# Eight experts on one core: the order of TensorE, ScalarE and VectorE written down, column-tile products side by side, weight splits one step ahead

## The chip, the core and the metric

One core of a Trainium2 chip runs the whole program. The metric is the device time of one execution in microseconds (us), lower is better. The kernel is one launch: two layers of a network on 256 tokens of width 1024. Layer 0 ends in a dense feed-forward net, layer 1 in eight experts. The change touches the experts alone.

## The reference, cut to what matters

```python
def moe_swiglu(h, w_router, w_up, w_down):            # h: 256 tokens x 1024
    logits = jnp.einsum('td,de->te', hf, w_router)
    top_logit, top_e = lax.top_k(logits, 2)           # two of eight experts for each token
    top_gate = jax.nn.softmax(top_logit, axis=-1)
    ...
    gate, up = jnp.split(h_pad[tok] @ w_up[e], 2, axis=-1)   # w_up[e]: 1024 x 7168
    return (jax.nn.silu(gate) * up) @ w_down[e]              # w_down[e]: 3584 x 1024
    ...
    out = zeros.at[slot_tok].add(slot_gate * y)
```

All weights are float32, and each expert's are read once: 8 x 42 parts of 1 MB.

## The kernel before

**Turns and blocks.** The experts are sorted by their number of tokens into turns 0 to 7. Turns 0, 1 and 2 have 128 rows (turn 1 up to 32 more, its "overflow"), turn 3 has 64, turns 4 to 7 have 32. A turn is 14 blocks of 256 hidden channels, and a block has three weight parts of 1 MB: two for the up product (U), one for the down product (D). Between U and D stands the gate step (G): silu times up, and a transpose through PSUM.

**The ring.** SyncE fetches the parts (`fetch`, L894) into a ring of ten 1 MB buffers in the order of `plan` (L887). The fetch of part n+10 waits until part n's buffer is free.

**Many rows (turns 0 to 2).** TensorE works with float32r, so a part is split in two halves into a high and a low piece: ScalarE copies (L257), VectorE subtracts (L258). A half goes into one of six pair buffers (`pairs`). Each product is then three matmuls (`mm3`, L252 to L254): 24 for a U, 12 for a D. A ring buffer is free once its part has been split. G transposes (L826) into the one PSUM bank `pb`, and `split` takes it from there.

**Few rows (turns 3 to 7 and the overflow).** The tokens are the stationary operand in column tiles of 32 or 64 (L1053 for U, L1075 and L1079 for D), and the weights stream unsplit in float32. A ring buffer is free only after its product. ScalarE takes U out of PSUM (L1055), TensorE transposes it into `pb` (L1062), ScalarE and VectorE gate it (L1066, L1067).

**The order.** `lanes_merged` mixes the blocks of the two lanes into one list of 112, mostly one many block (M) and then one or two few blocks (f): M f f M f M f f. `steps` (L1119 to L1138) does at step k, whatever the lane: U of block k, G of block k-1, D of block k-2, then `tick(2)`. A tick advances a queue of side jobs: `rows` gathers the next turn's tokens (VectorE L994, TensorE L1001, and L296 and L294 out of PSUM), `back` prepares its scatter matrix (L1014, L1018, L1020), and `scatter` adds a finished turn into x (TensorE L1040 into the one bank `pc`, VectorE L1042). In a scatter one tick adds the last product and issues the next one, which needs that bank. Before its scatter, `taken_out` (L1031) moves the turn's sums out of PSUM.

**Who sets each engine's order.** The whole of `lanes` is traced inside `manual_schedule` for TensorE alone: TensorE executes in the order of the trace. ScalarE and VectorE are ordered by the framework's scheduler. Each engine then works its list strictly in order.

Of the kernel before, what the change touches and what calls it, by code (L numbers as in the profile page):

```python
# [152 lines left out]
def trunk(tc, a, dbg=None):  # L153
# [83 lines left out]
    def halves(w, name, at=None):  # L237
        out = []
        for j in range(2):
            wj = w[:, 1024 * j:1024 * j + 1024]  # L240
            if at is not None:
                pair = pairs[taken[0] % PAIRS]
                taken[0] += 1
            else:
                pair = work.tile([P, 2, 1024], F32R, name=f"{name}{j}", tag="wp", bufs=count["wp"])
            with tc.issue_after(held.pop(0).ins) if held else ExitStack():
                split(pair[:, 0], pair[:, 1], wj)
            out.append((pair[:, 0], pair[:, 1]))
        return out

# [126 lines left out]
    def norm_affine(l, j, xn, scale=1.0):  # L377

        for q in range(2):
            n = slice(512 * q, 512 * q + 512)  # L380
            wb = []
            for r in range(2):
                t = base.tile([P, 512], F32, name="lnr", tag="lnr", bufs=2)
# [431 lines left out]
    def glu_products(ws, x_):  # L815
        p = bank("pa")
        for i, w in enumerate(ws):
            for k in (2 * i, 2 * i + 1):
                wh, wl = [t[:, 512 * (k % 2):512 * (k % 2) + 512] for t in w]
                mm3(p, *x_(k), wh, wl, k == 0, k == KD - 1)  # L820
        return glu_gate(p)

# [43 lines left out]
    def parts_in(order):  # L866
        for k in range(len(order) + 2):
            if k < len(order):
                yield from ((*order[k], i) for i in range(2))
            if k >= 2:  # L870
                yield (*order[k - 2], 2)
# [11 lines left out]

    def one_by_one():
        return [p for q in range(NE) for p in parts_in(blocks_of(q))]

    plan = list(parts_in(lanes_merged()))  # L887
    assert all(q == 0 for q, _, _ in plan[:RING]) and plan[:RING] == one_by_one()[:RING]
    ring, pairs, who, taken = [], [], [], [0]
# [11 lines left out]
    def moe(xn, cw, cb, g2):  # L901
# [87 lines left out]
        def rows(q, r, n, xe, xr, tag="pc"):  # L989

            rank, ind, _ = of_turn(q, r)
            sel = work.tile([P, NB, P], F32, name="sel")
# [14 lines left out]
        def back(q, r, n, pT):  # L1007
# [4 lines left out]
            wgt = work.tile([P, NB, P], F32, name="wgt")  # L1012
# [13 lines left out]
        def taken_out(n, ac):  # L1026

            ys = [base.tile([P, 512], F32, name="y_e", tag="lnr", bufs=2) for _ in range(2)] if n == P else [work.tile([P, 512], F32, name="y_f", bufs=2)] * 2
# [14 lines left out]


        def tiled_sums(n, ws, xr):

            m = P // n
            w = 512 // m
            ps = bank("pa")
# [4 lines left out]
            s = s2("pk", "aff")[:, 0:w]  # L1054
            A.copy(s, ps[:, 0:w])  # L1055
# [26 lines left out]
        def split_part(q, f, i):  # L1082

            n = plan.index((q, f, i))
            return ahead[n] if n in ahead else halves(ring[n % RING], "wup" if i < 2 else "mdn", True)

        def over_with(q, f, i):

            n = plan.index((q, f, i))
            if n + RING < len(plan):  # L1090
                fetch(n + RING)

        def used(q, f, which, parts, do):

            split_ = [w for i in which for w in split_part(q, f, i)] if any(p[0] == P for p in parts) else None
            tiled = any(p[0] < P for p in parts)
            if not tiled:
                for i in which:
                    over_with(q, f, i)
            tiles = [ring[plan.index((q, f, i)) % RING] for i in which]  # L1100
            out = [do(p, split_ if p[0] == P else tiles) for p in parts]
            if tiled:
                for i in which:
                    over_with(q, f, i)
            return out

        def steps(order, parts, at=lambda *step: None):


            taken[0] = 2 * AHEAD  # L1110
            ups, gs = {}, {}

            def up(p, ws):
                return glu_products(ws, lambda k: (p[1][:, k, :, 0], p[1][:, k, :, 1])) if p[0] == P else tiled_sums(p[0], ws, p[1])

            def gate_(q, u):
                return [glu_finish(v) if p[0] == P else tiled_gate(p[0], v) for p, v in zip(parts[q], u)]

            for k in range(len(order) + 2):  # L1119
                if k < len(order):  # L1120
# [5 lines left out]
                if k >= 2:  # L1126
                    q, f = order[k - 2]
                    of_part = {id(p): g for p, g in zip(parts[q], gs.pop(k - 2))}

                    def down(p, ws):  # L1130
                        if p[0] == P:
                            glu_down(p[2], of_part[id(p)], ws, f == 0, f == NEB - 1)
                        else:
                            tiled_down(p[0], p[2][0], of_part[id(p)], ws[0], f == 0, f == NEB - 1)
# [32 lines left out]
        def lanes():  # L1167

            order = lanes_merged()
# [12 lines left out]

            def at(step, q, f):
                lane = MANY if q in MANY else FEW
                if step == "up" and f == 0:
                    while coming.get(q) in queue:
                        tick()
                if step == "up" and f == 2 and q != lane[-1]:
                    prepare_turn(lane[lane.index(q) + 1])
                if step == "done" and f == NEB - 1 and order[-1] != (q, f):  # L1190
                    for i, (n, _, ac) in enumerate(parts[q]):
                        queue.append(scatter(n, taken_out(n, ac), pTo if i else place_of(q)[2]))

            prepare_turn(FEW[0])
            steps(order, parts, at)
            drain()
            q = order[-1][0]
            n, _, ac = parts[q][0]
            finish(n, taken_out(n, ac), place_of(q)[2])
# [26 lines left out]
        def alone(q, *ns):  # L1226
# [7 lines left out]
            steps(blocks_of(q), {q: parts})  # L1234
# [31 lines left out]
        ahead = {}  # L1266
        ahead.update({n: split_part(*plan[n]) for n in range(AHEAD)})
# [81 lines left out]
```

## Time and profile before

| | us |
|---|---|
| median of 3 runs | 1569.8 |
| lowest, highest | 1563.7, 1571.1 |
| profiled execution, its time | 1567.5 |
| profiled execution, span of the trace | 1565.7 |

Busy over the span: TensorE matmuls 86%, weight loads 64%, VectorE 60%, ScalarE 41%. Mean granted TensorE clock: 0.93 of full speed. Fetched: 481 MB. The profiled execution lies 1.8 us over its span and 2.3 us under the median. Matmuls are pipelined, so one that is recorded with 0.39 us can follow its neighbour after 0.23 us; a busy share of TensorE is therefore no measure of what is left. "A <- B" means that A waited for B.

### The profile page before, as it was taken

What the parts mean: (1) busy time and instruction counts of PE and PEld (TensorE: products, weight loads), DVE (VectorE), ACT (ScalarE), POOL (GpSimd) and SP (SyncE); (2) the same over time, 40 slices, a digit from 0 to 9 for tenths busy, and PEclk for the clock granted to TensorE, in tenths of its full rate; (3) what the DMA queues carried; (4) which work ended last, traced back from release to release, by engine and by line L of the source; (5) the groups of instructions that cost most, each with busy time, mean ns of one, the idle gap of its engine ahead of it and who ended that gap; (6) DMA issues with size and microseconds to landing.
All of it is one profiled execution on the core that took longest, in us unless ns stands there. A gap on an engine that the chain in (4) does not pass through costs nothing.

```text
span 1565.7 us, 26221 instructions
## 1 busy us (share of the span) xinstructions
PE 1351.9 (86%) x10468; PEld 1002.7 (64%) x10468; DVE 933.4 (60%) x1756; ACT 640.8 (41%) x1138; POOL 52.5 (3%) x44
## 2 busy tenths in 40 slices
PE   2799878999799997999989888888888898888884
PEld 2688756887688876776655656555656466655551
DVE  6799897888789968853433434344434544443433
ACT  2648733443465853652332323323423324433410
POOL 0000040000040003000000000000000000000000
PEclk9799979999989996999998898999999899989886
DMA  9772447889555215888999878897999989999994
GB/s 351 294 265 73 162 144 288 332 338 352 212 188 165 78 47 196 310 309 336 420 419 395 323 308 335 361 404 302 369 392 392 405 317 420 418 418 420 418 419 197
DMA packets 68755, 481.07 MB, mean 307 GB/s; under 512 B 8720, under 2 KB 8848, under 8 KB 11152
## 3 DMA queue, kind: packets, MB, share of 16 engines
q1 hardware_dynamic: 66672, 473.61, 76.7%
q0 software_dynamic: 960, 3.15, 0.7%
q10 hardware_dynamic: 992, 2.56, 0.4%
q8 instruction: 84, 1.38, 0.4%
q14 instruction: 47, 0.39, 0.1%
HBM read 478.23 MB, written 1.05 MB: 306 GB/s over the span
## 4 chain that ended last, share of the span: by engine, by line
PE 64%; DVE 16%; DMA 12%; ACT 5%; issue 3%; ACTq 0%; DVEq 0%; SPq 0%
PE pa L1053 10%; PE pa L253 7%; PE pa L254 7%; PE pa L252 7%; PE acc L253 5%; PE acc L254 5%; PE acc L252 4%; DMA rawb<-m_dn 4%; PE acc L1075 3%; DVE pair L258 3%; DMA rawb<-m_up 3%; DMA ring<-m_up 3%; DVE wada L327 2%; PE pc L1040 2%; PE pc L1001 2%
## 5 line engine op out<-in xcount | busy, mean ns | idle before, releaser
L258 DVE TENSOR_TENSOR pair<-rawb,pair 128x1024 fp32r<-128x1024 f32 x152 | 177.6, 1221 | 18.6 <-ACT pair L257 17.6
L257 ACT CAST pair<-rawb 128x1024 fp32r<-128x1024 f32 x152 | 149.4, 1048 | 14.0 <-DMA rawb<-m_up 4.6
L252 PE MATMUL pa<-pair,xe 128*128 128x512 f32 x336 | 141.1, 420 | 7.1 <-ACT xef L294 4.8
L253 PE MATMUL pa<-pair,xe 128*128 128x512 f32 x336 | 139.1, 414 | 6.5 <-DVE pair L258 6.5
L1055 ACT COPY pk<-pa 128x128 f32<-128x128 f32 (+1 forms) x84 | 23.8, 284 | 293.7 <-PE pa L1053 293.7
L254 PE MATMUL pa<-pair,xe 128*128 128x512 f32 x336 | 137.0, 408 | 0.0
L811 ACT ACTIVATE g_act<-pa 128x256 f32<-128x256 f32 x64 | 24.6, 385 | 245.6 <-PE pa L254 245.6
L258 DVE TENSOR_TENSOR pair<-ring,pair 128x1024 fp32r<-128x1024 f32 x100 | 117.0, 1223 | 12.0 <-ACT pair L257 11.9
L327 DVE CUSTOM_DVE_ANT_0 wada<-wada,sc 128x1024 f32<-128x1024 f32 x96 | 115.1, 1220 | 3.8 <-DMA wada<-w_ada 3.7
L258 DVE TENSOR_TENSOR g_l<-pb,g_h 128x256 fp32r<-128x256 f32 x64 | 27.1, 424 | 145.7 <-ACT g_h L257 145.6
L252 PE MATMUL acc<-pair,g_h 128*128 128x512 f32 x168 | 80.6, 480 | 35.5 <-ACT pair L257 35.5
L812 DVE TENSOR_TENSOR g_act<-g_act,pa 128x256 f32<-128x256 f32 x64 | 26.8, 419 | 136.6 <-ACT g_act L811 136.3
L257 ACT CAST pair<-ring 128x1024 fp32r<-128x1024 f32 x100 | 98.2, 1048 | 20.3 <-DVE rs_y L273 11.8
L1053 PE MATMUL pa<-rawb,xl 128*32 128x128 f32 (+1 forms) x2336 | 101.0, 294 | 1.4 <-DMA rawb<-m_up 1.4
L1053 PEld LDWEIGHTS pa<-rawb,xl 128*32 128x32 f32 (+1 forms) x2336 | 79.1, 116 | 35.1 <-issue 23.1
L253 PE MATMUL acc<-pair,g_h 128*128 128x512 f32 x168 | 82.2, 489 | 20.7 <-DVE pair L258 20.7
L1067 DVE TENSOR_TENSOR pk_g<-pk_g,pb 128x64 f32<-128x64 f32 (+1 forms) x84 | 19.3, 230 | 126.5 <-ACT pk_g L1066 126.5
L252 PEld LDWEIGHTS pa<-pair,xe 128*128 128x128 f32 x336 | 68.7, 204 | 36.2 <-ACT pair L257 12.6
L253 PEld LDWEIGHTS pa<-pair,xe 128*128 128x128 f32 x336 | 68.3, 203 | 23.1 <-DVE pair L258 9.2
L254 PE MATMUL acc<-pair,g_l 128*128 128x512 f32 x168 | 77.5, 461 | 0.0
L254 PEld LDWEIGHTS pa<-pair,xe 128*128 128x128 f32 x336 | 68.3, 203 | 14.1
L1053 PE MATMUL pa<-ring,xl 128*32 128x128 f32 (+1 forms) x1696 | 70.5, 296 | 6.6 <-DMA ring<-m_up 6.6
(320 smaller groups left out, 2838.4 us busy)
## 6 DMA issues: line engine op xcount, KB each, us to landing
rawb<-m_up SPq DMA_DIRECT2D x132, 1024.0 KB, 9.9
ring<-m_up SPq DMA_DIRECT2D x92, 1024.0 KB, 10.2
rawb<-m_dn SPq DMA_DIRECT2D x68, 1024.0 KB, 12.0
wada<-w_ada SPq DMA_DIRECT2D x48, 1024.0 KB, 6.6
ring<-m_dn SPq DMA_DIRECT2D x44, 1024.0 KB, 11.5
win<-w_in SPq DMA_DIRECT2D x24, 1024.0 KB, 5.3
wup<-f_up SPq DMA_DIRECT2D x22, 1024.0 KB, 5.8
fdn<-f_dn SPq DMA_DIRECT2D x11, 1024.0 KB, 6.0
```

The costliest lines, as they stand in the source:

```text
L252: T.matmul(ps, xh, wh, start=first, stop=False)
L253: T.matmul(ps, xh, wl, start=False, stop=False)
L254: T.matmul(ps, xl, wh, start=False, stop=last)
L257: A.copy(h, src)
L258: return V.tensor_sub(lo, src, h.bitcast(F32))
L327: V.tensor_tensor_reduce(wi, wi, sc, 1.0, 0.0, ALU.mult, ALU.add, c[:, i:i + 1])
L811: A.activation(g, p[:, 0:FB], AF.Silu)
L812: V.tensor_mul(g, g, p[:, FB:2 * FB])
L1001: T.matmul(ps[:, k * n:(k + 1) * n], xn[b][:, kk * P:(kk + 1) * P], sel[:, b, 0:n], start=b == 0, stop=b == NB - 1)
L1040: T.matmul(ps, pT[p, b], ys[h][p], start=True, stop=True)
L1053: T.matmul(ps[n * i:n * i + n, 0:w], xr[:, k], ws[k // 4][:, c:c + w], start=k == 0, stop=k == KD - 1)
L1075: T.matmul(ac[n * i:n * i + n], g[:, j], wd[:, D * j + 512 * h:D * j + 512 * h + 512], start=first, stop=last)
```

## The change

- The order of the work inside a step is written out by `in_lanes` as a program of (step, U/G/D, turn, block, part). In an f step it is: G of the last few block, G and U of the overflow, U of the new few block, D of the last few block and of the overflow, and then at its end the many lane's D and G if they are due. All column-tile products of a step then stand together. In an M step: the many lane's U, and those of its G and D that are due.
- `plan`, the fetch order, follows the new program: a few part D moves up by up to three places, many parts down by one.
- `split_until` emits the splits for the *next* step's many products right behind a U, ahead of the ScalarE step that takes that U out of PSUM, as far as the six pair buffers are free. The fetch into a split part's buffer is then also issued earlier.
- `manual_schedule` covers TensorE, ScalarE and VectorE: all three execute in traced order.
- One tick at the start of a step, and one more ahead of a many U, in place of two at the end of each step. A finished turn's scatter is queued only if at most three result buffers are in use; else ticks are run on the spot.
- Buffers: tag `lnr` has 3 instead of 2 and also holds `y_f`; `sel` and `wgt` share one buffer; the taken-out U has a tag of its own.

```diff
+    def in_lanes():
+        got = {w + k: [] for w in "UGD" for k in "mfo"}
...
+        for s in range(len(order) + 2):
+            q, f = order[s] if s < len(order) else (None, None)
+            if q in MANY:
...
+                put_(s, "U", "m")
+                fresh, got["Gm"] = got["Gm"], gated
+                put_(s, "G", "m")
+                later, got["Dm"] = got["Dm"], ready
+                put_(s, "D", "m")
...
+            else:
+                put_(s, "G", "f")
+                put_(s, "G", "o")
+                put_(s, "U", "o")
...
+                put_(s, "U", "f")
+                put_(s, "D", "f")
+                put_(s, "D", "o")
+                put_(s, "D", "m")
+                put_(s, "G", "m")
...
-            for k in range(len(order) + 2):
-                if k < len(order):
-                    q, f = order[k]
...
-                    ups[k] = used(q, f, (0, 1), parts[q], up)
-                if 1 <= k <= len(order):
-                    gs[k - 1] = gate_(order[k - 1][0], ups.pop(k - 1))
...
-                    used(q, f, (2,), parts[q], down)
-                    at("done", q, f)
-                tick(2)
+            def split_until(step, o):
+                while left[1] < len(todo):
+                    t = left[1]
+                    n, j, first, _ = todo[t]
+                    if program[first][0] > step or t >= PAIRS and todo[t - PAIRS][3] > o:
+                        return
+                    if t == len(ahead):
+                        ahead.append(half(ring[n % RING], j, pairs[t % PAIRS]))
...
+                    if j:
+                        released(n, [p for p in uses[n] if many(program[p])])
...
+                if what == "U":
+                    split_until(s + 1, o)
+                    sums[q, f, r] = glu_gate(ps) if n == P else tiled_take(ps)
...
+                if step == "next":
+                    tick()
+                elif step == "done":
+                    if q != end:
+                        n, _, ac = parts[q][f]
+                        while sum(u for t, u in sums if t in queue) + (2 if n == P else 1) > 3:
+                            tick()
...
+                    if q in MANY:
                         tick()
...
-            with tc.manual_schedule(engines={mybir.EngineType.PE}):
+            with tc.manual_schedule(engines={mybir.EngineType.PE, mybir.EngineType.Activation, mybir.EngineType.DVE}):
                 lanes()
```

## Rows read from the trace of the kernel before

**Rows 1.** Busy time by stage: us, busy of each engine, granted clock, DMA share, GB/s.

```profile
core 0: us, PE busy (x) PEld busy (x) DVE busy (x) ACT busy (x) POOL busy (x), PEclk, DMA share, GB/s
660.00:720.00 60.00, 57.18 (x344) 41.06 (x345) 27.39 (x50) 23.11 (x39) 0.00 (x0) 0.94 0.72 276
720.00:860.00 140.00, 130.30 (x759) 83.18 (x761) 51.93 (x64) 44.85 (x72) 0.00 (x0) 0.96 1.00 411
860.00:1000.00 140.00, 121.52 (x1304) 83.35 (x1301) 61.75 (x89) 48.37 (x84) 0.00 (x0) 0.91 0.81 321
1000.00:1060.00 60.00, 52.44 (x676) 35.58 (x674) 20.64 (x29) 16.72 (x32) 0.00 (x0) 0.94 0.99 403
1060.00:1080.00 20.00, 17.16 (x136) 10.86 (x132) 9.06 (x11) 6.83 (x11) 0.00 (x0) 0.91 0.51 187
1080.00:1220.00 140.00, 120.76 (x1577) 84.14 (x1568) 55.33 (x78) 51.02 (x93) 0.00 (x0) 0.97 0.96 390
1220.00:1300.00 80.00, 70.31 (x560) 44.73 (x560) 40.89 (x56) 25.48 (x41) 0.00 (x0) 0.92 0.92 363
1300.00:1543.00 243.00, 202.36 (x2119) 139.37 (x2117) 95.86 (x122) 78.03 (x131) 0.00 (x0) 0.89 1.01 417
```

**Rows 2.** Chain that ended last, its end: start us, us, what.

```profile
1523.77 19.33 DMA rawb<-m_dn
1543.23 1.10 PE acc L1075 x8
```

**Rows 3.** Waits of PE from 860 to 1300 us: us in total, times, longest.

```profile
PE acc L252 <- ACT pair L257: 16.6, 13, 1.5
PE pb L1062 <- DVE g_l L258: 12.9, 14, 0.9
PE acc L253 <- DVE pair L258: 11.7, 23, 0.8
PE pc L1040 <- DVE x L1042: 8.7, 10, 1.2
PE pa L253 <- DVE pair L258: 4.6, 5, 1.6
```

**Rows 4.** Timeline of ACT and PE, one many D: start us, us, [idle before].

```profile
1130.09 0.27 ACT L1055 COPY pk<-pa 128x128 f32<-128x128 f32 x1 [2.60 <-PE pa L1053]
1130.38 5.77 ACT L257 CAST pair<-rawb 128x1024 fp32r<-128x1024 f32 x6
1131.47 0.49 PE L252 MATMUL acc<-pair,g_h 128*128 128x512 f32 x1 [1.25 <-ACT pair L257]
1132.73 0.50 PE L253 MATMUL acc<-pair,g_h 128*128 128x512 f32 x1 [0.77 <-DVE pair L258]
1133.07 0.40 PE L254 MATMUL acc<-pair,g_l 128*128 128x512 f32 x1
1136.25 0.63 PE L253 MATMUL acc<-pair,g_h 128*128 128x512 f32 x1
```

**Rows 5.** Timeline of PE, two few steps between many products.

```profile
1146.38 1.07 PE L1075 MATMUL acc<-rawb,pk_g 128*32 128x512 f32 x8
1147.26 1.93 PE L1053 MATMUL pa<-rawb,xl 128*32 128x128 f32 x64
1149.12 0.44 PE L826 MATMUL pb<-small,g_act 128*128 128x128 f32 x2
```

**Rows 6.** Timeline: a D before a transpose, a many U's gate, a few block's gate.

```profile
1104.89 1.06 PE L1075 MATMUL acc<-ring,pk_g 128*32 128x512 f32 x8
1105.89 0.44 PE L1018 MATMUL pc<-small,wgt 128*128 128x128 f32 x2
1102.42 0.40 PE L254 MATMUL pa<-pair,xe 128*128 128x512 f32 x1
1103.27 0.42 DVE L812 TENSOR_TENSOR g_act<-g_act,pa 128x256 f32<-128x256 f32 x1 [2.88 <-ACT g_act L811]
1109.50 0.33 PE L1062 MATMUL pb<-small,pk 128*128 128x128 f32 x1 [0.92 <-DVE g_l L258]
1110.12 0.22 DVE L1067 TENSOR_TENSOR pk_g<-pk_g,pb 128x64 f32<-128x64 f32 x1 [0.68 <-ACT pk_g L1066]
```

**Rows 7.** DVE and ACT groups, 860 to 1300 us: busy, mean ns, idle before.

```profile
L258 DVE TENSOR_TENSOR pair<-rawb,pair 128x1024 fp32r<-128x1024 f32 x72 | 83.7, 1221 | 6.6 <-ACT pair L257 6.6
L1042 DVE TENSOR_TENSOR x<-x,pc 128x512 f32<-128x512 f32 x23 | 15.8, 687 | 26.0 <-PE pc L1040 25.9
L257 ACT CAST pair<-rawb 128x1024 fp32r<-128x1024 f32 x72 | 69.9, 1047 | 0.0
```

**Rows 8.** Timeline of PE, two scatter products in one pair of ticks.

```profile
1254.84 1.12 PE L1040 MATMUL pc<-y_f,pTo 64*128 64x512 f32 x2
1256.75 1.12 PE L1040 MATMUL pc<-y_f,pTo 64*128 64x512 f32 x2 [0.78 <-DVE x L1042]
```

More of the change, by code (lines that the diff above doesn't have):

```diff
@@ L235, in trunk, with halves, half @@
     held = []
-    def halves(w, name, at=None):
+    def halves(w, name):
         out = []
         for j in range(2):
[L240 to L248, printed above, removed]
-        return out
+            out.append(half(w, j, work.tile([P, 2, 1024], F32R, name=f"{name}{j}", tag="wp", bufs=count["wp"])))
+        return out
+    def half(w, j, pair):
+        with tc.issue_after(held.pop(0).ins) if held else ExitStack():
+            split(pair[:, 0], pair[:, 1], w[:, 1024 * j:1024 * j + 1024])
+        return pair[:, 0], pair[:, 1]
     def mm3(ps, xh, xl, wh, wl, first, last):
@@ L813, in glu_gate @@
         return g
[L815 to L821, printed above, removed]
     def glu_finish(g):
@@ L991, in rows @@
             rank, ind, _ = of_turn(q, r)
-            sel = work.tile([P, NB, P], F32, name="sel")
+            sel = work.tile([P, NB, P], F32, name="sel", tag="sel")
             for b in range(NB):
@@ L1026, in taken_out @@
         def taken_out(n, ac):
-            ys = [base.tile([P, 512], F32, name="y_e", tag="lnr", bufs=2) for _ in range(2)] if n == P else [work.tile([P, 512], F32, name="y_f", bufs=2)] * 2
+            ys = [base.tile([P, 512], F32, name="y_e", tag="lnr", bufs=3) for _ in range(2 if n == P else 1)]
+            ys = [ys[0], ys[-1]]
             for h in range(2):
@@ L1053, in tiled_sums, with tiled_take @@
                     T.matmul(ps[n * i:n * i + n, 0:w], xr[:, k], ws[k // 4][:, c:c + w], start=k == 0, stop=k == KD - 1)
-            s = s2("pk", "aff")[:, 0:w]
-            A.copy(s, ps[:, 0:w])
+            return ps[:, 0:w]
+        def tiled_take(ps):
+            s = work.tile([P, 256], F32, name="pk", bufs=2)[:, 0:ps.shape[1]]
+            A.copy(s, ps)
             return s
@@ L1080, in tiled_down @@
                                  start=first and j == 0, stop=last and j == 1)
[L1082 to L1105, printed above, removed]
@@ L1181, in prepare_turn @@
                     queue.append(coming[q])
+            sums = []
+            program = in_lanes()
+            end = program[-1][2]
             def at(step, q, f):
                 lane = MANY if q in MANY else FEW
-                if step == "up" and f == 0:
-                    while coming.get(q) in queue:
-                        tick()
[L1188 to L1192, printed above, removed]
+                if step == "next":
[5 more added lines that the diff above has]
+                            tick()
+                        sums.append((scatter(n, taken_out(n, ac), pTo if f else place_of(q)[2]), 2 if n == P else 1))
+                        queue.append(sums[-1][0])
+                else:
+                    if f == 0:
+                        while coming.get(q) in queue:
+                            tick()
+                    if f == 2 and q != lane[-1]:
+                        prepare_turn(lane[lane.index(q) + 1])
+                    if q in MANY:
+                        tick()
             prepare_turn(FEW[0])
-            steps(order, parts, at)
+            run(program, parts, at)
             drain()
-            q = order[-1][0]
-            n, _, ac = parts[q][0]
-            finish(n, taken_out(n, ac), place_of(q)[2])
+            n, _, ac = parts[end][0]
+            finish(n, taken_out(n, ac), place_of(end)[2])
         def finish(n=None, ys=None, pT=None):
@@ L1233, in alone @@
                 parts.append((n, to, accs[2 * r:2 * r + 2]))
-            steps(blocks_of(q), {q: parts})
+            run(in_turn(q, len(ns)), {q: parts})
             for (n, _, ac), pT in zip(parts, pTs):
@@ L1265, in moe @@
             pass
-        ahead = {}
-        ahead.update({n: split_part(*plan[n]) for n in range(AHEAD)})
+        first = [half(ring[t // 2], t % 2, pairs[t]) for t in range(2 * AHEAD)]
         take_turns()
         with tc.If(nc.values_load(cnt[0:1, 0, 0:1], min_val=0, max_val=1) > 0) as c:
-            with tc.manual_schedule(engines={mybir.EngineType.PE}):
+            with tc.manual_schedule(engines={mybir.EngineType.PE, mybir.EngineType.Activation, mybir.EngineType.DVE}):
                 lanes()
```

118 lines of the change are left out of this document (89 added, 29 removed).

## The prediction, made before the changed kernel was run

> **What bounds the kernel now.** I began with the stages [rows 1]. What to look at there is the rate of the fetches, not TensorE's busy share. From 1300 us on the fetch engines are full: 417 GB/s, DMA share 1.01. The chain of waits agrees: at its end it stands on one part's flight of 19.33 us, and the last few D starts 0.13 us after that lands [rows 2]. A part of 1.05 MB takes 2.51 us at 417 GB/s, so some eight parts are then under way at once, which is nearly the whole ring. In that stretch nothing that TensorE does faster can shorten the run. From 720 to 860 us it is the same, at 411 GB/s. From 860 to 1300 us it is not: the five stages move (140 x 321 + 60 x 403 + 20 x 187 + 140 x 390 + 80 x 363) / 440 = 356 GB/s [rows 1]. There the ring waits for its buffers, and so for TensorE, ScalarE and VectorE. At 417 GB/s the same bytes would need 440 x 356 / 417 = 376 us. **The room is 64 us**, and the change has to earn its gain from 860 to 1300 us. From 660 to 720 us the rate is low too (276 GB/s), but there TensorE is busy for 57.2 of 60 us, and the change removes no product; I count nothing.
>
> What TensorE waits for in the 440 us [rows 3] is mainly the splits: 16.6 us for ScalarE's copy and 11.7 us for VectorE's subtraction ahead of a many D, 4.6 us ahead of a U. One such place stands in [rows 4]. ScalarE stands idle for 2.60 us because its next instruction is the take-out of a few U, which isn't finished. Six weight copies are queued behind it. They start at 1130.38, and TensorE gets its first matmul of D at 1131.47, 1.25 us late, and the second 0.77 us late. The matmuls that followed at 0.40 us are then recorded at 0.63 us: the granted clock has fallen, which in these stages leaves it at 0.91 to 0.97 of full [rows 1], a mixture of 2.4 and 1.2 GHz.
>
> **The change, part by part,** from 860 to 1300 us, which in the list of 112 is about steps 32 to 79, with 18 many blocks.
>
> *Splits a step ahead, gain.* The copies now stand ahead of the take-out, so ScalarE works in the 2.60 us in which it was idle. The data are not the obstacle: outside the full stretches the parts have landed. I take all 16.6 + 11.7 + 4.6 = 33 us away. The splits stay beside TensorE's work: four halves need 4 x 1.22 us on VectorE [rows 7], and a few step with a many D lasts about 6 us.
>
> *Clock, gain.* (1 - clock) x length summed over the five stages is 12.6 + 3.6 + 1.8 + 4.2 + 6.4 = 29 us of lost pulses [rows 1]. Between nothing (the new waits below lower the clock as well) and 29 us, I take two thirds, 19 us, since the fall in [rows 4] follows just such a split wait.
>
> *Column-tile products side by side, gain.* From a few D to a column-tile U the start-to-start time is 0.88 us [rows 5], from a few D to a transpose over the whole array it is 1.00 us [rows 6]. A change of tiling thus costs 0.12 us. An M f f group had eight of them and will have four: 18 x 4 x 0.12 = 9 us.
>
> *One bank `pb`, cost.* G of the overflow now stands right behind G of a few block, and both use `pb`. Such a transpose starts at 1109.50, lasts 0.33 us, and VectorE has emptied the bank at 1110.34 [rows 6]: 0.5 us of waiting, 14 times, 7 us. The known wait for `pb` behind a many G (0.92 us, 12.9 us in all [rows 3]) stays where an f follows, and goes in the 4 blocks of turn 1 where an M follows: 3.7 us. Net 3 us.
>
> *Side jobs, cost; the term I know least.* In a tick TensorE waits for VectorE's addition before it may write `pc` again. Now that addition stands in the traced order behind everything of the step before, the next step's splits included. Behind a many U: its last matmul ends at 1102.82, the gate at 1103.69 [rows 6], the addition takes 0.69 us [rows 7], so 1.6 us. Behind a many G: 0.92 + 0.69 = 1.6 us. In the pair of ticks ahead of a many U: 0.78 us, as now [rows 8]. Worst is an M step behind a single f, where six splits stand in front: 1.05 + 6 x 1.22 us, then the many G's subtraction and the addition, some 10 us after the f step began, against 3.5 to 5.4 us that TensorE needs for it (D and U 0.88 and 1.86 us, start to start [rows 5]): 6.4 or 4.5 us. Written out, the steps in which a scatter is under way have five pairs (3.9), four ticks behind a U (6.2), one behind a G (1.6), three behind four splits (about 2), a run of forced ticks when turn 5 ends (2) and two of the worst kind (10.9): 27 us against 8.7 us now [rows 3], so 18 us more. For the five gathers I take 4 us more, between 0 and 8 (1.6 us each). Sum 22 us. From below it is nothing, if VectorE has run ahead; from above see the last rival.
>
> *Take-out behind the splits, cost.* In an M behind a single f of turn 1, the overflow's take-out now comes after six copies (6 x 1.05 us [rows 7]), and U waits for its PSUM bank: about 1.7 us, three times (the fourth is inside a tick's wait): 5 us.
>
> *At nothing:* the few D part fetched up to three places earlier is also used one step earlier; SyncE's earlier issues only lengthen its lead; the third `lnr` buffer serves GpSimd ahead of the experts; the end after the last landing is unchanged. When the fetches are the limit, a copy that waits for a part in flight now holds up the take-out and the next G. At most six landed parts then lie unused, and four of ten stay under way, still more than one at a time: cover enough.
>
> **Sum.** 33 + 19 + 9 = 61 us gained, 3 + 22 + 5 = 30 us lost, 31 us net. From 1000 to 1060 us the fetches are full already (0.99), 60 of 440 us, so I keep 86%: 27 us. The profiled execution's 1567.5 us (its span 1565.7 us and 1.8 us around it) less 27 is 1540.5; its 2.3 us to the median are within the spread of the runs. I forecast 1540 us.
>
> A rule that speaks against the change: the Trainium skill, "DMA: Bandwidth & Descriptors", section "Where 436 GB/s comes from", says that a transfer from HBM is bound at about 358 GB/s for each core. By it the 356 GB/s from 860 to 1300 us would be the limit already, the gain nothing and the time 1567 us, the second rival below. The trace speaks against it with 417 GB/s for 243 us [rows 1], so it adds no chance there.
>
> **Rivals.** *The whole room is won.* If VectorE and ScalarE run far enough ahead that the ticks cost no more than now, 61 - 3 - 5 = 53 us are there, and buffers freed a step earlier smooth the rest: at most 64 us, 1503 us. For it: VectorE is busy for 188 of the 440 us [rows 1]. Against it: six splits in one f step exceed that step. Chance 0.2, at 1503 to 1520.
>
> *Nothing is left.* The clock is not regained (19 us less) and the gathers cost their 8 us: 27 - 19 - 4 = 4 us, 1563 us; or the mean wait of a tick is 3 us. Chance 0.2, at 1562 to 1577.
>
> *Slower: VectorE's written order.* The side jobs' additions and affines outside the full stretches are some 20 on which TensorE waits. My sum has about 1.7 us for each. If four splits (4.9 us) stand in front each time, it is 20 x 3.2 = 64 us more: 1604 us. It decides from a mean of 1.7 + 27 / 20 = 3.0 us on. For it: in the old order the scheduler could put these short jobs first, and a split ahead may also wait for its part. Against it: ScalarE and VectorE stand idle for more than half of these stages. Chance 0.15, at 1578 to 1605.
>
> **How the numbers follow.** The forecast has 0.45, by itself 1525 to 1560. A measurement here tells 0.5%, about 8 us, from no change: the borders are 1562 and 1578. Faster is forecast and first rival, 0.65; same 0.2; slower 0.15. The range 1508 to 1590 leaves out about half of the first and of the last rival.
>
> **What would show it.** Right: from 860 to 1300 us the waits of a many D for the splits under 5 us in all (33 with U now), a rate above 375 GB/s, the granted clock at 0.95 or more, and the last landing near 1516 us. The waits of L1040 for L1042 grow, from 8.7 to some 27 us, the longest 4 to 6 us in an M step behind a single f; a wait of L1062 for L1067 of 0.5 us appears 14 times. Wrong: split waits that stay, or a rate under 356 GB/s; a full rate from 860 us on is the first rival, waits of L1040 and L1001 above 50 us in all are the last.

## The result, and the profile after

The changed kernel takes **1583.7 us** (median of 4 runs, 1582.2 to 1592.5) against 1567.3 us for the kernel before beside it: a ratio of 1.0116 with a 95% interval of 1.0069 to 1.0163. It is slower by 1.2%, where I had forecast 27 us faster. The time lies inside the range; the direction is wrong.

Line numbers have moved: splits are L254 (ScalarE) and L255 (VectorE), the scatter L1077 (TensorE) and L1079 (VectorE), the gather L1037, L293 and L291, a many G L815, a few U L1095, its take-out L1100, a few D L1120, a few block's transpose L1107 and its gate L1112. First the stages of the changed kernel, with the columns of [rows 1] and one stage more in front:

```profile
580.00:660.00 80.00, 65.24 (x293) 56.02 (x292) 57.70 (x137) 34.19 (x50) 13.08 (x10) 0.81 0.59 227
660.00:720.00 60.00, 57.70 (x324) 42.97 (x324) 28.86 (x45) 25.16 (x39) 0.00 (x0) 0.91 0.70 270
720.00:860.00 140.00, 130.28 (x791) 85.58 (x785) 59.05 (x75) 49.59 (x80) 0.00 (x0) 0.96 0.96 392
860.00:1000.00 140.00, 115.25 (x1262) 85.90 (x1266) 57.17 (x87) 44.76 (x82) 0.00 (x0) 0.90 0.83 333
1000.00:1060.00 60.00, 51.78 (x682) 38.19 (x674) 25.68 (x32) 21.36 (x38) 0.00 (x0) 0.94 0.99 406
1060.00:1080.00 20.00, 17.08 (x145) 10.76 (x149) 7.57 (x11) 4.99 (x9) 0.00 (x0) 1.00 0.99 407
1080.00:1220.00 140.00, 116.15 (x1556) 88.42 (x1548) 55.41 (x78) 48.63 (x89) 0.00 (x0) 0.94 0.92 372
1220.00:1300.00 80.00, 64.82 (x494) 40.84 (x498) 33.09 (x46) 20.14 (x33) 0.00 (x0) 0.83 0.81 325
1300.00:1543.00 243.00, 196.13 (x2039) 143.31 (x2028) 100.31 (x131) 80.45 (x137) 0.00 (x0) 0.88 0.99 407
```

The first of these stages in the kernel before, which I had not looked at:

```profile
580.00:660.00 80.00, 68.15 (x323) 58.74 (x321) 68.24 (x149) 40.98 (x57) 15.25 (x12) 0.85 0.69 262
```

Read as bytes, length times rate, the account closes (it has to, both kernels fetch the same parts); what it shows is where the bytes fall behind. From 580 to 860 us 89.2 MB came in against 95.1 MB before: 5.8 MB less, 14 us at 417 GB/s. From 860 to 1300 us it is 157.2 against 156.5 MB, a gain of not 2 us. From 1300 to 1543 us it is 407 against 417 GB/s, 2.4 MB or 6 us less. Together 18 us behind, and the last part lands 16.6 us later: at 1559.68 us, by the end of the chain of waits, against 1543.10 us [rows 2].

```profile
1542.20 17.48 DMA rawb<-m_dn
```

The waits of TensorE from 860 to 1300 us (us in total, times, longest) have changed their kind:

```profile
PE pc L1077 <- DVE x L1079: 27.9, 15, 6.0
PE pb L1107 <- DVE g_l L255: 21.6, 9, 6.1
PE pb L1107 <- DVE pk_g L1112: 8.2, 14, 0.8
PE pa L249 <- ACT pk L1100: 6.0, 3, 3.1
PE pc L1037 <- ACT xl L291: 3.1, 2, 1.6
```

No wait for a split is left (they were 33 us in [rows 3]). In its place stand the scatters (first line), `pb` behind a many G (second), and the small ones. One scatter of the worst kind, an M step behind a single f, in the timelines of VectorE, ScalarE and TensorE:

```profile
1273.46 2.36 DVE L255 TENSOR_TENSOR pair<-ring,pair 128x1024 fp32r<-128x1024 f32 x2 [0.71 <-ACT pair L254]
1275.74 4.62 DVE L255 TENSOR_TENSOR pair<-rawb,pair 128x1024 fp32r<-128x1024 f32 x4
1280.28 0.41 DVE L255 TENSOR_TENSOR g_l<-pb,g_h 128x256 fp32r<-128x256 f32 x1
1280.62 0.67 DVE L1079 TENSOR_TENSOR x<-x,pc 128x512 f32<-128x512 f32 x1
...
1274.28 3.88 ACT L254 CAST pair<-rawb 128x1024 fp32r<-128x1024 f32 x4
1278.06 0.26 ACT L1100 COPY pk<-pa 128x128 f32<-128x128 f32 x1
...
1274.91 0.44 PE L815 MATMUL pb<-small,g_act 128*128 128x128 f32 x2
1281.35 2.07 PE L1077 MATMUL pc<-y_e,pTl 64*128 64x512 f32 x2 [6.00 <-DVE x L1079]
1284.20 2.07 PE L1077 MATMUL pc<-y_e,pTl 64*128 64x512 f32 x2 [0.78 <-DVE x L1079]
1286.80 0.63 PE L250 MATMUL pa<-pair,xe 128*128 128x512 f32 x1
```

The addition that frees `pc` has had its operand since 1271.98 us (the product started at 1270.86 and lasted 1.12 us), but in the written order it stands behind six splits and the G's subtraction. TensorE stands for 6.00 us, and when it goes on it has lost its clock too: the product takes 2.07 us where [rows 8] has 1.12, and the first matmuls of U 0.63 instead of 0.39 us.

Something like it stands at the very start, where I had counted nothing. TensorE in the changed kernel, the two gather products around the first many U:

```profile
623.07 3.65 PE L1037 MATMUL pc<-sel,ln_xh 128*128 128x64 f32 x16 [3.43 <-DVE sel L1030]
636.09 3.57 PE L1037 MATMUL pc<-sel,ln_xh 128*128 128x64 f32 x16 [2.44 <-ACT xl L291]
```

In the kernel before, both stand without a wait and take 1.89 and 1.90 us (from 629.47 and 637.09 us), though its first many U has itself waited 4.82 us. In the run f3 below, in which the VectorE work for them stands elsewhere, they take as little:

```profile
629.78 1.89 PE L1037 MATMUL pc<-sel,ln_xh 128*128 128x64 f32 x16
637.39 1.90 PE L1037 MATMUL pc<-sel,ln_xh 128*128 128x64 f32 x16
```

Bytes run ahead of the work by up to a ring, so here is the work itself, by VectorE's gates of the 42 many blocks (L812 before, L809 after). The change is 17.4 us behind at the eighth (762.4 against 745.0 us), but only 2.4 us at the 28th, and 24.7 us at the last (1523.0 against 1498.3 us). The 28th, before and after:

```profile
1207.79 0.42 DVE L812 TENSOR_TENSOR g_act<-g_act,pa 128x256 f32<-128x256 f32 x1 [4.89 <-ACT g_act L811]
1210.23 0.42 DVE L809 TENSOR_TENSOR g_act<-g_act,pa 128x256 f32<-128x256 f32 x1 [8.42 <-ACT g_act L808]
```

So the change makes up what it lost at the start, and loses it again behind 1210 us: from 1220 to 1300 us the scatters wait 14.5 us, from 1300 to 1400 us `pb` waits 14.1 us behind a many G.

### The profile page after: what moved, and what is told of

Read it like the earlier page. It is cut to its first block, busy times and chain, and to the rows that moved or that the text cites. A ratio compares the mean times of both kernels' runs of the same rounds, so it can differ in the third digit from the quotient of the medians.

```text
span 1582.6 us, 26217 instructions
## 1 busy us (share of the span) xinstructions
PE 1336.1 (84%) x10468; PEld 1018.7 (64%) x10468; DVE 929.9 (59%) x1756; ACT 635.4 (40%) x1138; POOL 51.7 (3%) x44
## 4 chain that ended last, share of the span: by engine, by line
PE 57%; DVE 19%; DMA 15%; ACT 6%; issue 3%; ACTq 0%; DVEq 0%
PE pa L1095 8%; DMA rawb<-m_dn 8%; PE pa L249 6%; PE pa L250 6%; PE pa L251 6%; DMA ring<-m_dn 5%; DVE pair L255 5%; PE acc L249 4%; PE acc L250 4%; PE acc L251 4%; PE pc L1037 2%; PE acc L1120 2%; ACT pair L254 2%; DVE wada L324 2%; PE pc L1077 2%
## 5 line engine op out<-in xcount | busy, mean ns | idle before, releaser
L255 DVE TENSOR_TENSOR pair<-rawb,pair 128x1024 fp32r<-128x1024 f32 x150 | 174.7, 1219 | 63.2 <-ACT pair L254 63.1
L809 DVE TENSOR_TENSOR g_act<-g_act,pa 128x256 f32<-128x256 f32 x64 | 26.7, 418 | 282.7 <-ACT g_act L808 282.5
L254 ACT CAST pair<-rawb 128x1024 fp32r<-128x1024 f32 x150 | 147.3, 1047 | 38.8 <-DMA rawb<-m_dn 36.8
L249 PE MATMUL pa<-pair,xe 128*128 128x512 f32 x336 | 145.7, 434 | 6.0 <-ACT pk L1100 6.0
L255 DVE TENSOR_TENSOR pair<-ring,pair 128x1024 fp32r<-128x1024 f32 x102 | 119.7, 1225 | 44.5 <-ACT pair L254 44.5
L250 PE MATMUL pa<-pair,xe 128*128 128x512 f32 x336 | 140.3, 418 | 0.0
L251 PE MATMUL pa<-pair,xe 128*128 128x512 f32 x336 | 139.3, 415 | 0.0
L254 ACT CAST pair<-ring 128x1024 fp32r<-128x1024 f32 x102 | 100.1, 1046 | 41.4 <-DMA ring<-m_dn 22.5
L1095 PE MATMUL pa<-rawb,xl 128*32 128x128 f32 (+1 forms) x2336 | 110.0, 314 | 0.0
L1095 PEld LDWEIGHTS pa<-rawb,xl 128*32 128x32 f32 (+1 forms) x2336 | 84.3, 125 | 18.8 <-issue 6.7
L1107 PE MATMUL pb<-small,pk 128*128 128x128 f32 x98 | 29.1, 321 | 72.6 <-DVE g_l L255 64.3
L249 PEld LDWEIGHTS pa<-pair,xe 128*128 128x128 f32 x336 | 70.6, 210 | 28.3 <-issue 7.4
L250 PEld LDWEIGHTS pa<-pair,xe 128*128 128x128 f32 x336 | 70.3, 209 | 15.0 <-issue 1.0
L1095 PE MATMUL pa<-ring,xl 128*32 128x128 f32 (+1 forms) x1696 | 78.5, 322 | 1.6 <-DMA ring<-m_up 1.6
L251 PEld LDWEIGHTS pa<-pair,xe 128*128 128x128 f32 x336 | 69.7, 207 | 15.5
L1112 DVE TENSOR_TENSOR pk_g<-pk_g,pb 128x64 f32<-128x64 f32 (+1 forms) x84 | 19.3, 230 | 92.7 <-ACT pk_g L1111 92.5
L1107 PEld LDWEIGHTS pb<-small,pk 128*128 128x128 f32 x98 | 14.0, 149 | 91.6 <-DVE g_l L255 70.4
L254 ACT CAST win<-win 128x1024 fp32r<-128x1024 f32 x48 | 49.9, 1055 | 56.3 <-PE acc L251 25.9
L250 PE MATMUL pa<-wup,hTf 128*128 128x512 f32 x176 | 70.1, 398 | 2.4 <-DVE wup L255 2.4
L1095 PEld LDWEIGHTS pa<-ring,xl 128*32 128x32 f32 (+1 forms) x1696 | 61.2, 129 | 14.1 <-issue 3.4
```

The source lines that it names most:

```text
L249: T.matmul(ps, xh, wh, start=first, stop=False)
L250: T.matmul(ps, xh, wl, start=False, stop=False)
L251: T.matmul(ps, xl, wh, start=False, stop=last)
L254: A.copy(h, src)
L255: return V.tensor_sub(lo, src, h.bitcast(F32))
L809: V.tensor_mul(g, g, p[:, FB:2 * FB])
```

## The experiments

Theories, once the result was known. **S, side jobs:** a tick's VectorE part stands in the written order behind splits that TensorE doesn't need yet, while its TensorE part stands at the head of the step; TensorE pays the difference, and at the start of the experts too. **T, order of TensorE:** the new step program itself is worse. **L, late part:** a split a step ahead waits for a part still in flight and holds up whatever is behind it. Ratios are to the kernel before on the same chip:

| run | us | ratio, 95% interval |
|---|---|---|
| the change | 1583.7 | 1.0116, 1.0069 to 1.0163 |
| e1_sched | 1553.9 | 0.9915, 0.9884 to 0.9946 |
| e2_no_ahead | 1593.9 | 1.0173, 1.0135 to 1.0212 |
| e3_behind_g | 1593.6 | 1.0170, 1.0133 to 1.0208 |
| e4_tick_mid | 1538.3 | 0.9817, 0.9771 to 0.9862 |
| f1_mid_sched | 1533.9 | 0.9775, 0.9753 to 0.9797 |
| f2_mid_no_ahead | 1564.1 | 0.9968, 0.9954 to 0.9981 |
| f4_mid_late_d | 1531.5 | 0.9762, 0.9742 to 0.9782 |
| f3_two_halves | 1512.7 | 0.9638, 0.9606 to 0.9671 |
| g3_scatter_halves | 1550.3 | 0.9895, 0.9875 to 0.9916 |
| g4_halves_no_ahead | 1521.7 | 0.9706, 0.9686 to 0.9725 |
| g2_halves_sched | 1509.9 | 0.9625, 0.9599 to 0.9651 |
| g1_halves_late_d | **1501.7** | 0.9579, 0.9551 to 0.9607 |

### Which part of the change costs

**e1_sched**: ScalarE and VectorE go back to the framework's order.

```diff
-            with tc.manual_schedule(engines={mybir.EngineType.PE, mybir.EngineType.Activation, mybir.EngineType.DVE}):
+            with tc.manual_schedule(engines={mybir.EngineType.PE}):
```

> The changed kernel with one line undone: only TensorE's order is taken from the trace, ScalarE and VectorE are ordered by the scheduler again. Theory S (side jobs: the additions and affines stand behind splits in VectorE's written order) and theory L (late part: the take-out and the many G's cast stand behind a split whose part has not landed, so that the next G waits for its bank) both lie in the written order of the two engines and expect some 20 to 40 us less than the changed kernel, 1545 to 1563 us, the waits for bank pb behind g_l (64 us) down to under 25 us and those for bank pc (some 55 us with the gathers) under 30 us. Theory T (the new order of TensorE and of the fetches costs the time itself) expects 1575 us or more.

30 us faster than the change, and faster than the kernel before, so T falls as the cause: all that the change does besides is worth some 13 us. S and L both expected this; e1 doesn't tell them apart. Its waits from 640 us on show the trade, scatters down from 31.0 to 10.3 us, split waits back:

```profile
PE acc L250 <- DVE pair L255: 19.2, 38, 2.4
PE acc L249 <- ACT pair L254: 13.6, 10, 2.5
PE pc L1077 <- DVE x L1079: 10.3, 9, 4.1
```

**e2_no_ahead**: no splits a step ahead.

```diff
-                    split_until(s + 1, o)
```

> The changed kernel without splits ahead: a part is split only ahead of the product that uses it; the three written orders stay. Theory L expects the pb waits behind g_l to fall from 64 us to about 20 us, but the split waits come back at 1.05 + 1.22 us or more for each many product, some 84 x 2.3 us in all: 1600 us or more. Theory S expects the waits for pc to fall from 31 to about 15 us, since no split stands ahead of the next tick. Both expect a slower kernel than the changed one; if it is as fast or faster, splitting ahead is itself the loss.

Some 10 us slower than the change by the medians, but the intervals overlap (from 1.0135 to 1.0163). If the splits ahead are a gain in this kernel, it is far from the 33 us of my ledger. L had expected 1600 us or more; the `pb` waits behind a many G fall to 19.6 us, as it said. The scatters wait 21.4 us, where S had said about 15.

**e3_behind_g**: the splits of a many D due in an f step go to that step's start; only a many U's are made a step ahead.

```diff
                 if s != before:
                     at("next", q, f)
+                    split_until(s, o - 1)
...
-                    split_until(s + 1, o)
+                    if s + 1 in leads:
+                        split_until(s + 1, o)
```

> The changed kernel with one emission moved: the two splits of a many D that is due in an f step are emitted at that step's start, behind the many G of the f step before, and no longer ahead of that step's take-out. Splits ahead of an M step stay where they are. Theory L expects the pb waits behind g_l to fall from 64 to about 15 us (the 0.9 us ones stay) and 1565 to 1575 us. Theory S expects no more than 5 us: 1579 us or more, with the waits for pc as they are (31 us for the additions).

L had expected it faster (1565 to 1575 us), and it isn't; whether it is slower, overlapping intervals leave open. The long waits of `pb` behind a many G are gone (19.6 us left from 640 us on, none over 0.9), but a few block's gate now stands behind the splits, and the scatters wait as before:

```profile
PE pc L1077 <- DVE x L1079: 32.3, 19, 6.0
PE acc L1120 <- DVE pk_g L1112: 30.7, 11, 7.6
PE pb L1107 <- DVE pk_g L1112: 28.2, 14, 3.1
```

So this run doesn't clear L: it moves the blockage to another waiter.

**e4_tick_mid**: the ticks go behind the step's first U, ahead of the splits.

```diff
                 if what == "U":
+                    if s not in ticked:
+                        ticked.add(s)
+                        at("mid", q, r)
                     split_until(s + 1, o)
...
-                    tick()
+                    pass
+                elif step == "mid":
+                    tick(2 if q in MANY and f == 0 else 1)
...
-                    if q in MANY:
-                        tick()
```

> The changed kernel with the ticks moved: one tick behind the first U of an f step and two behind the U of an M step, ahead of the splits for the next step, in place of one at the start of each step and one ahead of a many U. Theory S expects the waits of L1040's product for L1042's addition (31 us) under 12 us, those of the gathers (17 us) under 6 us, the first U of turn 0 and of turn 3 some 10 us earlier, and 1550 to 1565 us. Theory L expects no more than 5 us: 1579 us or more, with the 64 us for pb as they are.

The number of ticks is that of the change: `at` gets r here, which is 0 for a turn's own rows, so every M step has two. 45 us faster by moving a few lines: S, and by more than it had expected (1550 to 1565 us). The scatters wait 6.2 us, the gathers 7.1 us (under 6 was expected), and most of what is left stands in one line, from 640 us on:

```profile
PE pb L1107 <- DVE g_l L255: 81.5, 27, 8.2
PE pc L1077 <- DVE x L1079: 6.2, 8, 0.8
```

### With the ticks moved: what the other parts are worth

**f1_mid_sched**: e4 and e1 together.

> The kernel with the ticks behind U (e4_tick_mid, 1538 us), but ScalarE and VectorE ordered by the scheduler. If the written order of the two engines is worth something of itself once the side jobs stand well, this is slower by the split waits that come back (33 us of waiting in e1_sched): 1545 to 1560 us. If the written order only did harm that the ticks repaired, it is as fast or faster: 1525 to 1540 us.

Its interval overlaps e4's, as the second expectation has it: once the ticks stand right, writing out ScalarE and VectorE neither gains nor costs what can be measured.

**f2_mid_no_ahead**: e4 and e2 together.

> The kernel with the ticks behind U (1538 us), without splits ahead: a part is split only ahead of its product. Between the changed kernel and e2_no_ahead the splits ahead were worth 10 us. If side jobs and splits add up, this comes to about 1548 to 1560 us; if the splits ahead carry most of the gain once the side jobs are out of the way, to 1570 us or more; if they are worth nothing, to 1535 to 1542 us.

Without the splits ahead 24 us are lost by the ratios, 26 by the medians, between the first two expectations: here they are worth nearly what I had given them (33 us, 28 after the share for full stretches). But most of it lies where I had not looked: up to 860 us f2 has fetched 85.9 MB and e4 93.2 MB, 7.3 MB or 18 us; from 860 to 1300 us it is 168.2 against 171.9 MB, 9 us.

**f4_mid_late_d**: e4, with the splits of a many D that is due in the second f step put between that step's G and its U.

```diff
-                if n == P:
+                if n == P or what == "U":
                     split_until(s, o - 1)
+                if n == P:
...
-                    split_until(s + 1, o)
+                    if s + 1 in leads:
+                        split_until(s + 1, o)
```

> The kernel with the ticks behind U (1538 us), and the two splits of a many D that is due in a second f step emitted in that step, between its G and its U, no longer ahead of the take-out of the step before. The waits for bank pb behind g_l (81 us) should fall below 30 us. If they cost time of themselves, the kernel gets faster, at most by the rest of the room, some 10 us from 860 to 1300 us: 1525 to 1533 us. If they stand where the fetches are the limit anyway, it stays within 4 us of 1538.

7 us by the medians, but the intervals overlap by 0.001; the `pb` waits fall from 81.5 to 24.9 us. Most of those 57 us are not saved, since other waits take their place: added up from 640 us on, all waits of TensorE go from 115.1 to 106.2 us. g1 asks again.

### The tick cut in two

**f3_two_halves**: each tick becomes a pair. Its VectorE and ScalarE part ("V") stands behind the step's first U, ahead of the splits; the TensorE part ("T") at the start of the next step. One pair for each step, in the gathers as in the scatters; an M step thus has one pair where the change and e4 have two ticks. What that alone is worth was not tried.

```diff
-        def tick(n=1):
-            for _ in range(n):
-                while queue and next(queue[0], queue) is queue:
-                    queue.pop(0)
+        part = {}
+        def tick(kind=None):
+            while queue and kind in (None, part.setdefault(queue[0], "V")):
+                part[queue[0]] = next(queue[0], None)
+                if part[queue[0]]:
+                    return
+                queue.pop(0)
...
                     T.matmul(ps, pT[p, b], ys[h][p], start=True, stop=True)
-                    yield from LAG
+                    yield "V"
                     V.tensor_add(x[:, b, c], x[:, b, c], ps)
...
                 if step == "next":
-                    tick()
+                    tick("T")
+                elif step == "mid":
+                    tick("V")
```

> The changed kernel with each tick cut in two, one pair for each step: VectorE's and ScalarE's part (addition, affine, copy) is emitted behind the step's first U, ahead of the splits for the next step; TensorE's part (product, transpose) stays at the start of the step, where the change has it. Theory S names VectorE's order: it expects the waits for bank pc (31 us for the additions, 17 us for the gathers) under 6 us in all and 1530 to 1545 us. If the place of TensorE's product were what costs, the time would stay at 1575 us or more.

71 us faster than the change, 54 faster than the kernel before, and 17 us faster than S had expected at best, with the same three engines written out and the same products. Two of its stages (its lines L1079 to L1122 are those of the change plus 2):

```profile
580.00:660.00 80.00, 71.66 (x354) 60.94 (x354) 64.10 (x145) 38.06 (x56) 13.06 (x10) 0.89 0.65 248
660.00:720.00 60.00, 60.00 (x382) 44.98 (x380) 31.42 (x52) 27.61 (x46) 0.00 (x0) 1.00 0.91 357
```

and its waits from 640 us on:

```profile
PE pb L1109 <- DVE g_l L255: 75.7, 23, 8.4
PE pc L1079 <- DVE x L1081: 2.0, 2, 1.2
```

The scatters wait 2.0 us for additions (and 6.7 us for the sums that `taken_out` moves, 6.8 us in the change), and no gather waits at all. From 660 to 720 us the rate is 357 GB/s, where the kernel before had 276 [rows 1] and I saw TensorE too busy for any gain: but it was busy for 57.2 us at clock 0.94, and in f3 for 60.0 us at 1.00. That is some 12% more clock for a rate 29% higher; part of the rest comes with the splits ahead, for in g4 below, without them, the rate there is 320 GB/s.

**g3_scatter_halves**: the change with the scatters alone cut in two; gathers stay at the starts of steps and ahead of a many U (their yields become "G", which `at("next")` and the many U's tick run).

> The change, with the scatters alone cut in two halves (addition behind the first U, product at the next step's start); the gathers stay at the starts of steps and ahead of a many U as in the change. It divides the loss of 71 us (1583.7 against 1512.7) between the two kinds of side job. If scatters make nearly all of it, as the waits from 860 to 1300 us say (27.9 us against some 11 of the gathers), 1520 to 1530 us, with the start-up as late as in the change (U3 near 662 us). If the gathers at start-up count in full, because the fetches set the end from there on and 15 us lost by U3 never come back, 1535 to 1550 us.

By the ratios the scatters make 2.2% (1.0116 less 0.9895, 35 us), the gathers 2.6% (0.9895 less 0.9638, 40 us). The time stands at the upper edge of the second expectation: 8.6 us of gather waits from 860 to 1300 us in the change (xl, wgt, xef) don't explain 40 us; the start explains most. g3 still has it:

```profile
580.00:660.00 80.00, 66.18 (x291) 56.90 (x290) 56.76 (x137) 33.81 (x49) 12.93 (x10) 0.79 0.59 225
660.00:720.00 60.00, 57.53 (x320) 42.62 (x322) 28.39 (x44) 25.13 (x40) 0.00 (x0) 0.91 0.70 267
720.00:860.00 140.00, 131.84 (x799) 87.69 (x796) 59.72 (x76) 50.12 (x80) 0.00 (x0) 0.95 0.95 391
```

Up to 860 us this is 88.8 MB against f3's 99.1 (413 GB/s from 720 to 860 us): 10.3 MB, 25 us at 417 GB/s. By the work done it is the same: the seventh many gate stands 26 us later in g3 than in f3, the last one 33 us.

**g4_halves_no_ahead**: f3 without the splits ahead (e2's edit).

> f3 without the splits a step ahead. If the splits ahead are worth what my ledger gave them (33 us of waits and part of the clock), it is 26 to 40 us slower than f3: 1539 to 1553 us, with 40 to 65 us of waits of acc and pa for the split back. If most of f3's gain is the place of the side jobs alone, and it needs no splits ahead, under 1525 us.

Only 9 us slower than f3 (11 by the ratios), with 62.5 us of split waits back:

```profile
PE acc L250 <- DVE pair L255: 24.4, 48, 2.4
PE acc L249 <- ACT pair L254: 18.4, 12, 2.5
PE pb L1109 <- DVE g_l L255: 16.4, 18, 0.9
PE pa L250 <- DVE pair L255: 10.0, 14, 0.8
PE pa L249 <- ACT pair L254: 9.7, 9, 1.4
```

The first expectation was some three times too high; the second (under 1525 us, most of the gain is the place of the side jobs) is met. The third line shows what the splits ahead cost: f3 pays 75.7 us there, g4 16.4. By stages, g4 has fetched 93.8 MB up to 860 us against f3's 99.1, 13 us less, and from 860 to 1300 us 177.1 against 174.1, 7 us more.

**g2_halves_sched**: f3 with e1's edit.

> f3 with ScalarE and VectorE ordered by the framework again, TensorE alone written. If the written order of ScalarE and VectorE is worth nothing of itself once side jobs stand where TensorE's list wants them (f1 against e4: 4 us faster without it), 1505 to 1516 us. If it is the written order that turns the halves into the gain, the split waits of e1 come back (45 us in all) and it goes to 1530 us or more.

Level with f3 (the intervals overlap), as f1 is with e4. Split waits of 54.8 us are back and the `pb` waits down to 18.9 us: the scheduler trades one for the other. The first expectation holds.

**g1_halves_late_d**: f3 with f4's edit.

> Ticks cut in two as in f3 (1512.7 us), and the splits of a many D that is due in the second f step stand between that step's G and its U instead of ahead of the take-out in the step before. If copies that wait for a part in flight still cost time (f3 has 75.7 us of waits of pb for g_l), about 7 us are won as in f4 against e4: 1505 us, and those waits fall below 35 us. If those waits only stand where the fetches set the end (f3 fetches at 399 to 418 GB/s from 720 us on), it stays at 1510 to 1516 us though the waits fall.

The fastest of all, 66 us below the kernel before. All its 4 runs (1497.2 to 1504.5) lie under all 4 of f3 (1509.0 to 1517.2), on another chip; the intervals of the ratios just touch (0.9606 and 0.9607). The waits of `pb` fall from 75.7 to 16.4 us, all waits of TensorE together from 105.0 to 98.4 us (U's wait for the overflow's take-out grows from 6.0 to 18.7 us), and the fetches run full in nearly every stage:

```profile
860.00:1000.00 140.00, 123.99 (x1557) 92.63 (x1557) 67.25 (x95) 57.09 (x98) 0.00 (x0) 0.96 0.99 407
1080.00:1220.00 140.00, 122.24 (x1444) 86.69 (x1442) 63.43 (x84) 48.67 (x84) 0.00 (x0) 0.95 1.01 414
1220.00:1300.00 80.00, 67.73 (x705) 48.49 (x701) 35.64 (x51) 28.72 (x48) 0.00 (x0) 0.96 1.01 418
```

So L holds, at about 10 us in f3, and the 7 us in e4 agree; and splits ahead, placed so that they block less, are worth 20 us here (g4 against g1, 1.3%).

## Why the prediction was wrong

**What held.** *Splits a step ahead:* the 33 us of waits are gone, to nothing. *Side jobs:* I wrote out 27 us for the scatters and the trace has 27.9; the worst kind was put at 6.4 or 4.5 us and measures 6.00 in the case shown. *One bank `pb`:* 14 waits, 7 us forecast, 8.2 measured. *Take-out behind the splits:* 5 us, three times; measured 6.0, three times. The gathers wait 8.6 us where they waited 1.0, near the upper end of what I allowed. The end after the last landing is the same. These waits were seen, with their place and size, and still the sum had the wrong sign. Against the forecast of 27 us gained, the bytes say 18 us lost; of the 45 us between, 25 lie from 860 to 1300 us (27 forecast, under 2 won), 14 ahead of it and 6 behind. Three steps failed.

**1. "I count nothing" from 660 to 720 us.** The room was looked for only where the rate was low and TensorE had idle time. The stage from 580 to 660 us wasn't read at all, and gathers were priced only from 860 us on. The change puts a gather product ahead of the first many U and another behind four splits and a gate; the waits are 3.43 and 2.44 us, the products run at half speed (3.65 and 3.57 us against 1.89), and 14 us of fetches are lost by 860 us. What the gathers lose there is not won back of itself: between g3 and f3 it is 26 us at the seventh many gate and 33 us at the last. In the change against the kernel before, other gains make it up by the 28th gate, and the two losses behind 1210 us undo that. The place hides a gain as well: f3 fetches 4.0 MB more than the kernel before up to 860 us, 10 us at 417 GB/s. "TensorE is busy for 57.2 of 60 us" was read as a limit although the clock beside it was 0.94, and although splits ahead raise the rate there too (320 GB/s in g4, 357 in f3).

**2. "Clock, gain: 19 us."** The sum of (1 - clock) x length over the five stages went from 29 to 14 + 3.6 + 0 + 8.4 + 13.6 = 40 us: 11 us lost where I had 19 gained, a term off by 30 us, as large as the whole net. My reason was that split waits make the clock fall. They did in [rows 4], but they were short (at most 1.6 us [rows 3]), and what took their place is fewer and longer. The range "between nothing and 29 us" shut out a loss, though the text itself said that the new waits lower the clock. That the waits cause the lower clock is read from places like the one at 1281 us; no run changed the clock alone. Nor is the sum a price in time: in f3, read in the same five stages, it is 36 us, more than before, and all waits of TensorE there are 55.9 us against 57.8, yet f3 fetches 174.1 MB in them against 156.5. In the change waits (57.8 to 74.7 us) and clock got worse by 28 us, and still 0.7 MB more came in. So the ledger of waits and clock misses a gain that both have; no run shows what it is.

**3. "At nothing": a copy that waits for a part in flight.** I argued that four of ten parts stay under way, and that outside the full stretches "the parts have landed". In the kernel before they had: from 860 to 1300 us ScalarE's copies waited for no part. In the change, where the copies stand a step earlier, they do:

```profile
ACT pair L254 <- DMA rawb<-m_dn: 19.6, 4, 6.7
```

The bytes of these stages are level with before (157.2 and 156.5 MB); but VectorE and ScalarE stand behind the copy, and so does the many G's subtraction that frees `pb`: 21.6 us from 860 to 1300 us where I had carried 9.2 (12.9 less 3.7), and from 1300 us on, where I looked for nothing,

```profile
PE pb L1107 <- DVE g_l L255: 36.5, 8, 9.4
```

What it costs in the change itself no run isolates (e3 moved it to another waiter); between f3 and g1 it is some 10 us, between e4 and f4 7 us.

**The rivals.** "VectorE's written order" named the side of the result and its mechanism, and its time (1578 to 1605 us) holds it, with a chance of 0.15. Its condition was not met: the mean wait of a tick in the scatters is 27.9 / 15 = 1.9 us, not 3.0, and the waits of scatter and gather products from 860 to 1300 us are 27.9 + 3.1 + 2.7 = 33.7 us, not over 50. Of the rows that I had named as proof, the rate (357 GB/s, short of 375) and the clock (under 0.95 in four of five stages) spoke against the forecast, and the last landing came at 1560 instead of 1516 us. e1 shows that the written order costs 30 us in this kernel; f3 and g2 show that it isn't the writing: with the side jobs' halves in place, written or scheduled makes no difference that can be measured. The first rival, the whole room won, was 1503 to 1520 us; f3 and g1 (1501.7 us) are what it looks like. The room was well drawn: against the kernel before, g1 fetches 23.3 MB more from 860 to 1300 us, 56 of the 64 us (f3: 17.6 MB, 42 us); another 10 us lie ahead of 860 us, outside it.

**Still open.** The splits ahead are worth 26 us beside e4's ticks and 9 or 10 us in the change and in f3. Up to 860 us they bring much the same in all three, 7.3, 6.6 and 5.3 MB more (13 to 18 us); from 860 to 1300 us they add 3.7 MB in e4 and cost 4.8 and 3.0 MB in the change and in f3. The `pb` waits explain that only in part, since e4 has them too (30.8 us; 21.6 in the change, 39.0 in f3). The column-tile grouping was not tried alone: my 9 us for it are unproved, and it is one candidate for the gain that the ledger misses. Nor was the number of ticks in an M step.

## What to carry over

When an order is written out for engines that work strictly in order, place a short job that another engine waits for by its consumer: its VectorE half ahead of the long work that can wait, its TensorE half a step later. A whole tick at the head of a step joins both at the worst place; moving it was worth 45 us, moving and cutting it in two 71 us, while the splits ahead brought 9 to 26 us by what stood around them. And read the ledger from the first fetched byte: 5.9 us of waits around the first many U, and the lower clock behind them, are where the change began to fall behind, by 17 us at its eighth many block; and a busy share next to a clock under 1.00 is no proof of a limit.

## What the runs showed of the hardware

One gather product of 16 matmuls takes 1.89 us after work without a gap and 3.65 us after a wait of 3.43 us, nearly the ratio of 2.4 to 1.2 GHz; a wait can thus cost the work behind it as well. It need not: in the kernel before, a gather product of 16 matmuls (128x128) took 1.95 us without a wait (656.26 us) and 2.05 us after a wait of 2.45 us (660.65 us), while in the change the same product took 3.38 us after 1.93 us (659.67 us). No run shows what decides. And 419 GB/s held for 160 us in g1:

```profile
1300.00:1460.00 160.00, 128.81 (x1312) 89.18 (x1312) 66.49 (x82) 54.42 (x87) 0.00 (x0) 0.88 1.01 419
```

The clock there is 0.88, the lowest of g1's stages from 580 us on, and no fetch is lost to it: the DMA share is 1.01.
